# Side work of an RWKV-7 branch in fewer, larger steps: where pieces of it stand between the projection matmuls

## The chip, the cores and the metric

The kernel runs on one core of one Trainium2 chip. The metric is the device time of one execution in microseconds (us). Five engines work beside each other, each on its own queue of instructions in a fixed order: PE (TensorE, matmuls; PEld is its weight load), DVE (VectorE), ACT (ScalarE), POOL (GpSimd) and SP (SyncE, which here issues weight loads). An engine whose next instruction waits holds everything behind it.

## The reference

One decoder layer for x of 256 rows and 2048 columns, float32. A normalised x is projected once into all inputs of two branches, RWKV-7 time mixing (16 heads of 64) and block-sparse attention ("MoBA", 16 heads of 64); both are gated, projected to 2048, merged with sigmoid gates, and one output projection is added to x. The part that the change touches is the recurrence of RWKV-7. Cut to what matters:

```python
def step(state, inp):
    r_t, w_t, k_t, v_t, kk_t, b_t = inp
    sa = jnp.einsum('bhvk,bhk->bhv', state, -kk_t)
    state = (state * w_t[:, :, None, :] + sa[..., None] * b_t[:, :, None, :]
             + v_t[..., None] * k_t[:, :, None, :])
    y_t = jnp.einsum('bhvk,bhk->bhv', state, r_t)
    return state, y_t
_, y = lax.scan(step, state0, xs)
# group norm of y per head, then:
bonus = jnp.sum(rh * kh * r_k.reshape(H, N), axis=-1, keepdims=True) * vh
```

The kernel does not run 256 steps: it works in 4 chunks of 64 rows. For a chunk it needs the products of all keys with all receivers inside the chunk (key products), the inverse of a triangular matrix made of them, the values and keys transposed, and the sum over a head for the bonus (head sums).

## The kernel before

**Jobs.** The weights are float32 and each is split into a high part (`hi`) and the rest (`lo`), so that a product of precision takes three matmuls. The unit is a job: one half of a 1 MB weight load (`raw`, two buffers, one load feeds two jobs). For a job ACT makes `hi` (L216), DVE makes `lo = raw - hi` (L222), and PE runs 24 matmuls of 256 columns (L329) or 12 of 512 (L347 to L349). `hi` and `lo` have three buffers each. 258 jobs follow each other, numbered from 0: first the RWKV inputs of head group g=0 (heads 0 to 7) and attention's inputs, jobs 0 to 49; the same for g=1, jobs 50 to 97; then gates from job 98 on (98 to 129 with L329), the projections of the branches and the output projection. `run_jobs(look)` prepares job i (load, `hi`, `lo`) two jobs ahead of the one whose matmuls it issues, and after the matmuls of each job it calls `pump()`.

**Side work.** Everything else is written as Python generators in one queue, `rwkv_elem`, `rwkv_r`, `rwkv_mid`, `rwkv_v` for RWKV and `moba` for attention, per head group. `pump()` takes one step, up to the next `yield`, of the generator that stands first. So a `yield` sets how much side work is written between two jobs. A scheduler that knows dependencies and buffers then orders the instructions per engine; it can place a piece inside the matmuls of a job or some jobs away. Two steps written as one are written into one gap.

**The generators at the change.** `rwkv_r` makes the key products: for each of four feature tiles `fi` 8 matmuls into two PSUM tiles (L534; each shows as two in the trace), which DVE copies under a mask into `LL` (L538), and a `yield`. Then 16 small DMAs from ACT's queue write blocks of `LL` to DRAM (`gd`, L549), and one DMA gathers them into `sg` (L551), 64 small matrices of 32 by 32. `inverse` solves these with 31 pairs of DVE instructions on `tmp` and `kk` (L566, L569), two pairs a step; the first pair waits for `sg`. It ends with a DMA to DRAM, `td` (L573), and four that bring it back in another layout, `cs` (L578). `merge` uses `cs`: DVE transposes (L586), PE products (L595), ACT copies, PE products again. `rwkv_tr` runs in step with `inverse` (`zipped`: one step of each per gap): transposes of values on PE (L622), copied by ACT into `UV` (L628); head sums on PE (L401), multiplied with the values by DVE into `yaT` (L635, L639); transposes of keys on PE (L645), copied by ACT into `BK` (L647). It had 2 + 2 + 3 steps beside 20 of `inverse`. `rwkv_mid` is one step, then the two together, then `merge`.

**PSUM.** All small results use the pool `psd` with four buffers (tag `ps`); a fifth tile waits until the first has been read. The main matmuls have four of their own (`pm`).

Of the kernel before, what the change touches and what calls it, by code (L numbers as in the profile page):

```python
# [36 lines left out]
def tile_hybrid_block(ctx: ExitStack, tc: tile.TileContext, x, pv, wdu, wau,  # L37
# [13 lines left out]
    def nm(s):  # L51
        cnt[0] += 1
        return f"{s}_{cnt[0]}"

    def T(tag, shape, dt=F32, bufs=1):
        return sb.tile(shape, dt, tag=tag, name=nm(tag), bufs=bufs)
# [4 lines left out]
    def PSS():  # L61
        return psd.tile([P, 512], F32, tag="ps", name=nm("ps"))
# [4 lines left out]
    def f32(ap):  # L67
        return ap.bitcast(F32)
# [327 lines left out]
    def head_sums(ps, parts, half):  # L396

        for i in range(2):
            fs = slice((2 * half + i) * S, (2 * half + i + 1) * S)
            for u in range(2):  # L400
                pe.matmul(ps[:, i * S:(i + 1) * S], bones, parts[u][:, fs], start=(u == 0),  # L401
                          stop=(u == 1))
# [108 lines left out]
    def rwkv_r(g):  # L511
        r = R[g]
        rr, k, ep, ar, bk = r["r"], r["k"], r["ep"], r["ar"], r["bk"]
        dve.tensor_tensor(ar[:, :, :, 1, :], rr.rearrange("p f (c t) -> p f c t", c=4),
                          ep[:, :, :, 1:65], ALU.mult)
        yield
        for fi in range(4):
            col = 4 * g + fi
            dve.scalar_tensor_tensor(rr[:, fi, :], rr[:, fi, :], PV[:, PV_RK + col:PV_RK + col + 1],
                                     k[:, fi, :], ALU.mult, ALU.mult)  # L520
        yield
        rv = rr.rearrange("p f t -> p (f t)")
        rh, rl = T("a", [P, 1024], F32R), T("cs", [P, 1024], F32R)
        act.activation(rh, rv, AF.Copy)
        dve.tensor_tensor(rl, rv, f32(rh), ALU.subtract)
        r["rr"] = (rh, rl)
        yield
        for fi in range(4):

            pss = [PSS() for _ in range(2)]  # L530
            for c in range(4):
                for p in range(2):
                    sl = slice(64 * p, 64 * p + 64)
                    pe.matmul(pss[p][:, c * P:(c + 1) * P],  # L534
                              bk[sl, fi, c].rearrange("p a t -> p (a t)"),
                              ar[sl, fi, c].rearrange("p a t -> p (a t)"), start=True, stop=True)
            for p in range(2):
                dve.copy_predicated(  # L538
                    LL[p][:, fi].rearrange("p c a t -> p c (a t)"),
                    m2.rearrange("p a t -> p (a t)").rearrange("p (o t) -> p o t", o=1)  # L540
                    .to_broadcast([P, 4, P]),
                    pss[p].rearrange("p (c t) -> p c t", c=4))
            yield
        G = T("sg", [64, 32, 32])
        gd = dp.tile([4, 4, 4, 32, 32], F32, tag="gd", name=nm("gd"))
        for b in range(4):
            h = b % 2
            for fi in range(4):
                act.dma_start(gd[b, fi].rearrange("c s t -> s c t"),  # L549
                              LL[b // 2][32 * b:32 * b + 32, fi, :, 0, 32 * h:32 * h + 32])  # L550
        act.dma_start(G, gd.rearrange("b f c s t -> (b f c) s t"))  # L551
        Ti = T("kk", [64, 32, 32])
        pool.memset(Ti, 0.0)
        pool.memset(Ti.rearrange("p a b -> p (a b)")[:, 0:1024:33], 1.0)
        r["G"], r["Ti"] = G, Ti
# [55 lines left out]
    def rwkv_tr(g):  # L611
        r = R[g]
        v, bk, rr = r["v"], r["bk"], r["r"]
        UV = T("UV", [P, 4, 2, 4, 64])
        BK = T("BK", [P, 3, 512])
        r["UV"], r["BK"] = UV, BK
        pool.memset(UV[0:64, :, 0], 0.0)
        pool.memset(UV[64:128, :, 1], 0.0)
        for cp_ in range(2):
            ps = PSS()  # L620
            for fi in range(4):
                pe.transpose(ps[:, fi * P:(fi + 1) * P], v[:, fi, cp_ * P:(cp_ + 1) * P], ident)  # L622
            p4 = ps.rearrange("q (f p e) -> q f p e", f=4, p=2)
            for cc in range(2):
                sl = slice(64 * cc, 64 * cc + 64)
                for p in range(2):
                    so = slice(64 - 64 * p, 128 - 64 * p)
                    act.activation(UV[so, 2 * cp_ + cc, p], p4[sl, :, p, :], AF.Copy)  # L628
            yield
        for half in range(2):  # L630
            ps = PSS()
            fs = slice(2 * half, 2 * half + 2)
            head_sums(ps, r["rr"], half)
            ya = yaT[:, 4 * g + 2 * half:4 * g + 2 * half + 2, :]
            dve.tensor_tensor(ya.rearrange("p f t -> p (f t)"),  # L635
                              v[:, fs, :].rearrange("p f t -> p (f t)"), ps, ALU.mult)
            for i in range(2):
                col = 4 * g + 2 * half + i
                dve.tensor_scalar(ya[:, i, :], ya[:, i, :], PV[:, PV_GB + col:PV_GB + col + 1], None,  # L639
                                  ALU.add)  # L640
            yield
        for c in range(3):
            ps = PSS()
            for fi in range(4):
                pe.transpose(ps[:, fi * P:(fi + 1) * P],  # L645
                             bk[:, fi, c].rearrange("p a t -> p (a t)"), ident)
            act.activation(BK[:, c, :], ps, AF.Copy)  # L647
            yield

    def zipped(a, b):  # L650
        live = [a, b]
# [9 lines left out]
    def rwkv_mid(g):  # L661
        yield
        yield from zipped(inverse(g), rwkv_tr(g))
        yield from merge(g)
# [373 lines left out]
    for g in range(2):  # L1038
        c = 512 * g
        chunk(w_in, C_K + c, 512, KT, fm_x, shift_post("k", "k", g, PV_MUK, 8))  # L1040
        post = shift_post("r", "r", g, PV_MUR, 0)
        if g == 0:
            chunk(w_in, C_WD, 128, KT, fm_x, then(wa_post, (rwkv_elem(0), "e0")))
        else:
            post = then(post, (rwkv_elem(1), "e1"))
        chunk(w_in, C_R + c, 512, KT, fm_x, then(post, (rwkv_r(g), f"r{g}")))
        vp = then(shift_post("v", "v", g, PV_MUV, 16), (rwkv_mid(g), f"i{g}"), (rwkv_v(g), f"v{g}"))
        chunk(w_in, C_V + c, 512, KT, fm_x, with_need("v0", vp) if g else vp)
        qp = qk_post("q", g)
        chunk(w_in, C_Q + c, 512, KT, tm_x, with_need("m0", qp) if g else qp)  # L1050
        chunk(w_in, C_KQ + c, 512, KT, tm_x, qk_post("k", g))
        chunk(w_in, C_VQ + c, 512, KT, tm_x, then(vq_post(g), (moba(g), f"m{g}")))
# [63 lines left out]
```

## Time and profile before

| | |
|---|---|
| three runs | 831.91 us median, 829.71 to 832.96 |
| profiled execution, whole time | 834.34 us |
| its span, first to last instruction | 832.6 us |
| mean granted TensorE clock | 0.999 of full speed |
| busy PE, DVE, ACT, POOL | 819.9, 551.9, 417.8, 29.9 us |
| DMA | 145.78 MB, 175 GB/s mean |

A busy share says how much of the span an engine worked. The timeline gives each instruction with the idle time of its engine ahead of it and what ended that; a small arrow names the releaser. For an engine that is busy nearly all the time, the brackets are what is left to gain, and the room in front of other brackets is what can be lost. "ACTq" and "SPq" rows are DMAs being issued by those engines, not their transfers.

### The profile page before, as it was taken

The numbers are of one execution on the slowest core, as the hardware profiler recorded it, in microseconds if no ns is written. First come the engines' busy times: TensorE is split into PE (matmuls) and PEld (weight loads), VectorE is DVE, ScalarE is ACT, GpSimd is POOL, SyncE is SP. The second block draws the span as 40 slices with busy tenths as digits, with TensorE's granted clock in tenths as the row PEclk, the third lists the DMA queues.
The fourth block names the chain that finished last, engine by engine and source line by source line (L and its number), as shares of the span: only waits on it lengthen the run. The fifth ranks groups of instructions, "written<-read, shape, count | busy, mean of one in ns | idle before, by whom it ended". The sixth has DMA issues, their size and how long they took to land.

```text
span 832.6 us, 15909 instructions
## 1 busy us (share of the span) xinstructions
PE 819.9 (98%) x6770; PEld 764.4 (92%) x6770; DVE 551.9 (66%) x776; ACT 417.8 (50%) x565; POOL 29.9 (4%) x42
## 2 busy tenths in 40 slices
PE   8999999999999999999999999999999999999998
PEld 7999778899998888999999999999999999998887
DVE  5869958956569679649974588644445566665453
ACT  6785446444437784444444487444344444443332
POOL 5001100000000003000000000000000000000000
PEclk9999999999999999999999999999999999999999
DMA  8564554654434544655673424655555555556772
GB/s 305 181 201 152 180 166 160 202 177 153 136 119 131 174 146 137 210 140 178 203 228 106 149 66 143 224 189 172 198 194 169 195 193 166 199 182 202 248 232 97
DMA packets 83206, 145.78 MB, mean 175 GB/s; under 512 B 11568, under 2 KB 13872, under 8 KB 83136
## 3 DMA queue, kind: packets, MB, share of 16 engines
q1 hardware_dynamic: 71584, 138.55, 51.2%
q10 hardware_dynamic: 11520, 6.16, 2.8%
q8 instruction: 53, 0.87, 0.4%
q14 instruction: 17, 0.14, 0.0%
q0 software_dynamic: 32, 0.05, 0.0%
HBM read 141.61 MB, written 3.15 MB: 174 GB/s over the span
## 4 chain that ended last, share of the span: by engine, by line
PE 90%; DMA 3%; DVE 3%; ACT 2%; issue 1%; ACTq 0%; SPq 0%; DVEq 0%
PE pm L329 55%; PE pm L348 9%; PE pm L347 9%; PE pm L349 9%; PE ps L534 1%; PE ps L672 1%; PE ps L679 1%; DMA cs<-td 1%; DMA sg<-gd 1%; DVE lo L222 1%; DMA td<-kk 1%; PE ps L878 1%; DMA raw<-in_w_in_dram 1%; PE ps L696 1%; PE ps L831 1%
## 5 line engine op out<-in xcount | busy, mean ns | idle before, releaser
L222 DVE TENSOR_TENSOR lo<-raw,hi 128x1024 fp32r<-128x1024 f32 (+1 forms) x259 | 314.4, 1217 | 211.8 <-ACT hi L216 210.9
L216 ACT ACTIVATE hi<-raw 128x1024 fp32r<-128x1024 f32 (+1 forms) x259 | 272.4, 1055 | 343.9 <-PE pm L329 195.9
L329 PE MATMUL pm<-xh,hi 128*128 128x256 f32 x1168 | 329.0, 283 | 1.1 <-ACT xh L144 1.1
L329 PE MATMUL pm<-xh,lo 128*128 128x256 f32 x1168 | 325.4, 280 | 3.6 <-DVE lo L222 3.6
L329 PE MATMUL pm<-xl,hi 128*128 128x256 f32 x1168 | 326.1, 280 | 0.0
L329 PEld LDWEIGHTS pm<-xh,hi 128*128 128x128 f32 x1168 | 221.2, 190 | 4.5 <-ACT xh L144 1.5
L329 PEld LDWEIGHTS pm<-xh,lo 128*128 128x128 f32 x1168 | 219.8, 189 | 4.7 <-DVE lo L222 4.5
L329 PEld LDWEIGHTS pm<-xl,hi 128*128 128x128 f32 x1168 | 219.7, 189 | 0.5
L348 PE MATMUL pm<-lo,xh 128*128 128x512 f32 x192 | 76.5, 398 | 0.0
L349 PE MATMUL pm<-hi,xl 128*128 128x512 f32 x192 | 75.5, 393 | 0.0
L347 PE MATMUL pm<-hi,xh 128*128 128x512 f32 x192 | 72.6, 398 | 0.0
L348 PE MATMUL pm<-lo,mgh 128*128 128x512 f32 (+1 forms) x128 | 48.4, 378 | 0.0
L349 PE MATMUL pm<-hi,mgl 128*128 128x512 f32 (+1 forms) x128 | 48.1, 376 | 0.0
L347 PE MATMUL pm<-hi,mgh 128*128 128x512 f32 (+1 forms) x128 | 44.4, 378 | 0.0
L348 PEld LDWEIGHTS pm<-lo,xh 128*128 128x128 f32 x192 | 36.1, 188 | 8.0 <-DVE lo L222 0.8
L349 PEld LDWEIGHTS pm<-hi,xl 128*128 128x128 f32 x192 | 36.1, 188 | 7.3
L347 PEld LDWEIGHTS pm<-hi,xh 128*128 128x128 f32 x192 | 35.9, 188 | 7.5
L347 PEld LDWEIGHTS pm<-hi,mgh 128*128 128x128 f32 x128 | 24.1, 188 | 4.7
L349 PEld LDWEIGHTS pm<-hi,mgl 128*128 128x128 f32 x128 | 24.0, 188 | 4.7
L348 PEld LDWEIGHTS pm<-lo,mgh 128*128 128x128 f32 x128 | 24.1, 188 | 4.4
L566 DVE TENSOR_TENSOR tmp<-sg,kk 64x31 f32<-64x31 f32 (+15 forms) x62 | 20.5, 330 | 10.4 <-DMA sg<-gd 9.2
L329 PE MATMUL pm<-bk,hi 128*128 128x256 f32 x128 | 22.8, 281 | 0.0
(275 smaller groups left out, 983.5 us busy)
## 6 DMA issues: line engine op xcount, KB each, us to landing
raw<-in_w_in_dram SPq DMA_DIRECT2D x94, 1024.0 KB, 5.1
raw<-in_w_out_dram SPq DMA_DIRECT2D x16, 1024.0 KB, 5.4
raw<-in_w_proj_moba_dram SPq DMA_DIRECT2D x8, 1024.0 KB, 5.1
raw<-in_w_proj_rwkv_dram SPq DMA_DIRECT2D x8, 1024.0 KB, 5.1
raw<-in_w_in_dram SPq DMA_DIRECT2D x5, 512.0 KB, 6.1
k<-in_x_dram ACTq DMA_DIRECT2D x4, 256.0 KB, 4.0
r<-in_x_dram ACTq DMA_DIRECT2D x4, 256.0 KB, 4.2
k<-in_x_dram SPq DMA_DIRECT2D x2, 256.0 KB, 4.9
```

Of the source, the lines that this page charges most:

```text
L216: act.activation(job["hi"][:, c], job["src"][:, c], AF.Copy)
L222: dve.tensor_tensor(job["lo"][:, c], job["src"][:, c], f32(job["hi"][:, c]), ALU.subtract)
L329: pe.matmul(o, (hi, hi, lo)[ps][:, i, cs], (mh, ml, mh)[ps](k), start=(k == 0 and fi % 2 == 0 and ps == 0), stop=(k == jb["last"] and ps = ...
L347: pe.matmul(o, sh[:, k, ts], hi[:, i, cs], start=(k == 0), stop=False)
L348: pe.matmul(o, sh[:, k, ts], lo[:, i, cs], start=False, stop=False)
L349: pe.matmul(o, sl[:, k, ts], hi[:, i, cs], start=False, stop=end)
L534: pe.matmul(pss[p][:, c * P:(c + 1) * P], bk[sl, fi, c].rearrange("p a t -> p (a t)"), ar[sl, fi, c].rearrange("p a t -> p (a t)"), start= ...
L566: dve.tensor_tensor(tv, gcol.to_broadcast([64, nt, j + 1]), trow.to_broadcast([64, nt, j + 1]), ALU.mult)
L672: pe.matmul(ps[64 * p:64 * p + 64, c0 + 64 * fi:c0 + 64 * fi + 64], LL[p][:, fi, c, which, :], UV[:, c, p, fi, :], start=(fi == 0), stop=( ...
L679: pe.matmul(ps[sl, c0 + 64 * fi:c0 + 64 * fi + 64], ar[sl, fi, c, which, :], St[sl, fi, :], start=False, stop=True, skip_group_check=True)
L696: pe.matmul(ps[sl, cols], X64[sl, fi * 4 + c, :], Zs[sl, cols], start=True, stop=True)
L831: pe.matmul(pss[p][:, i * nk:(i + 1) * nk], q[rows, fi, 0:P] if u == 0 else q[rows, fi, P:S], k[rows, fi, 0:nk], start=True, stop=True)
```

## The change

Three `yield`s move. In `rwkv_r` the step ends after two feature tiles in place of one, so that four PSUM tiles of key products are written in one gap and the generator has 5 steps in place of 7. In `rwkv_tr` the two transposes of values, the two head sums and the three transposes of keys are one step each: 3 steps in place of 7. As `inverse` still has 20 steps and runs beside it, `rwkv_mid` has as many steps as before. No instruction's work is changed. Behind L543 the lines of the changed kernel are one higher (L552 there is L551 here).

```diff
@@ rwkv_r @@
                     pss[p].rearrange("p (c t) -> p c t", c=4))
-            yield
+            if fi % 2:
+                yield
         G = T("sg", [64, 32, 32])
@@ rwkv_tr @@
                     act.activation(UV[so, 2 * cp_ + cc, p], p4[sl, :, p, :], AF.Copy)
-            yield
+        yield
         for half in range(2):
...
                 dve.tensor_scalar(ya[:, i, :], ya[:, i, :], PV[:, PV_GB + col:PV_GB + col + 1], None,
                                   ALU.add)
-            yield
+        yield
         for c in range(3):
...
             act.activation(BK[:, c, :], ps, AF.Copy)
-            yield
+        yield
```

Where instructions stand now is seen in the order per engine. First ACT's queue for g=1, before, around the gather `sg` (`hi` of jobs 106, 107 and 108; the number behind a name tells buffers apart):

```order
L549 DMA gd_3889<-LL_7_120 32x4x32 x2
L549 DMA gd_3889<-LL_8_121 32x4x32 x2
L216 ACTIVATE hi_3912<-raw_3818 128x1024
L216 ACTIVATE hi_3959<-raw_3818 128x1024
L551 DMA sg_3888<-gd_3889 64x1024
L628 ACTIVATE UV_3946<-ps_3950 64x256 x4
L216 ACTIVATE hi_4013<-raw_3910 128x1024
```

The same place now; the `hi` rows are those of jobs 101, 102, 103 and 104:

```order
L216 ACTIVATE hi_3744<-raw_3623 128x1024
L550 DMA gd_3773<-LL_8_121 32x4x32
L550 DMA gd_3773<-LL_7_120 32x4x32 x2
L550 DMA gd_3773<-LL_8_121 32x4x32
L550 DMA gd_3773<-LL_7_120 32x4x32 x2
L550 DMA gd_3773<-LL_8_121 32x4x32 x3
L216 ACTIVATE hi_3796<-raw_3688 128x1024
L552 DMA sg_3772<-gd_3773 64x1024
L216 ACTIVATE hi_3852<-raw_3688 128x1024
L629 ACTIVATE UV_3830<-ps_3834 64x256 x4
L629 ACTIVATE UV_3830<-ps_3843 64x256 x4
L216 ACTIVATE hi_3904<-raw_3794 128x1024
```

The gather stands behind one `hi` where it stood behind two, and both sets of copies of values stand together behind the next.

DVE at the start of the inverse of g=1, before (`lo` of jobs 106, 107, 108; L170 and the `k` rows belong to gates):

```order
L222 TENSOR_TENSOR lo_3914<-raw_3818,hi_3912 128x1024
L222 TENSOR_TENSOR lo_3961<-raw_3818,hi_3959 128x1024
L566 TENSOR_TENSOR tmp_3940<-sg_3888,kk_3907 64x31
L170 TENSOR_TENSOR k_3987<-pm_3666,rbc 128x512
L569 TENSOR_TENSOR kk_3907<-kk_3907,tmp_3940 64x31
L170 TENSOR_TENSOR k_3987<-pm_3667,rbc 128x512
L566 TENSOR_TENSOR tmp_3943<-sg_3888,kk_3907 64x60
L569 TENSOR_TENSOR kk_3907<-kk_3907,tmp_3943 64x30x2
L222 TENSOR_TENSOR lo_4015<-raw_3910,hi_4013 128x1024
```

And now (`lo` of jobs 103 and 104 at the ends; L636 is the multiplication of the head sums):

```order
L222 TENSOR_TENSOR lo_3854<-raw_3688,hi_3852 128x1024
L567 TENSOR_TENSOR tmp_3824<-sg_3772,kk_3791 64x31
L570 TENSOR_TENSOR kk_3791<-kk_3791,tmp_3824 64x31
L567 TENSOR_TENSOR tmp_3827<-sg_3772,kk_3791 64x60
L570 TENSOR_TENSOR kk_3791<-kk_3791,tmp_3827 64x30x2
L567 TENSOR_TENSOR tmp_3880<-sg_3772,kk_3791 64x87
L570 TENSOR_TENSOR kk_3791<-kk_3791,tmp_3880 64x29x3
L567 TENSOR_TENSOR tmp_3883<-sg_3772,kk_3791 64x112
L636 TENSOR_TENSOR yaT<-v_3028,ps_3886 128x512
L570 TENSOR_TENSOR kk_3791<-kk_3791,tmp_3883 64x28x4
L636 TENSOR_TENSOR yaT<-v_3028,ps_3894 128x512
L222 TENSOR_TENSOR lo_3906<-raw_3794,hi_3904 128x1024
```

Seven small instructions of the inverse and the first multiplication now stand between the wait for `sg` and the point where the PSUM tile of the first head sums is read. On PE the key transposes of g=1 stood one set at a time, with a job's matmuls between (ahead of and behind the first of three):

```order
L329 MATMUL pm_4018<-xl,hi_4013 128x256
L329 MATMUL pm_4018<-xh,lo_4015 128x256
L645 MATMUL ps_4135<-ident,bk_3597 128x128 x4
L329 MATMUL pm_4017<-xh,hi_4057 128x256
L329 MATMUL pm_4017<-xl,hi_4057 128x256
```

Now all three stand between the matmuls of job 102 (`hi_3796`) and of job 103 (`hi_3852`):

```order
L329 MATMUL pm_3695<-xl,hi_3796 128x256
L329 MATMUL pm_3695<-xh,lo_3798 128x256
L646 MATMUL ps_3938<-ident,bk_3563 128x128 x4
L646 MATMUL ps_3944<-ident,bk_3563 128x128 x4
L646 MATMUL ps_3950<-ident,bk_3563 128x128 x4
L329 MATMUL pm_3694<-xh,hi_3852 128x256
```

The third of them takes the PSUM buffer that the first head sums had. Last, ACT at the end of the inverse of g=1, before (`hi` of jobs 126 to 129):

```order
L216 ACTIVATE hi_4681<-raw_4619 128x1024
L216 ACTIVATE hi_4713<-raw_4619 128x1024
L573 DMA td_4545<-kk_3907 64x1024
L216 ACTIVATE hi_4779<-raw_4679 128x1024
L578 DMA cs_4547<-td_4545 32x16x32 x4
L216 ACTIVATE hi_4843<-raw_4679 128x1024
```

And now (`hi` of jobs 121 to 124):

```order
L216 ACTIVATE hi_4524<-raw_4436 128x1024
L216 ACTIVATE hi_4554<-raw_4494 128x1024
L574 DMA td_4429<-kk_3791 64x1024
L216 ACTIVATE hi_4586<-raw_4494 128x1024
L579 DMA cs_4431<-td_4429 32x16x32 x4
L946 ACTIVATE qsq_4615<-qkn_4614 128x512
L216 ACTIVATE hi_4661<-raw_4552 128x1024
```

Before, `td` stood behind the second `hi` of one weight load (`raw_4619` twice); now it stands behind the first of one (`raw_4494`), and the second follows.

## Rows read from the trace of the kernel before

**Rows 1.** The profile page, busy time by engine, and granted clock in 40 slices

```profile
PE 819.9 (98%) x6770; PEld 764.4 (92%) x6770; DVE 551.9 (66%) x776; ACT 417.8 (50%) x565; POOL 29.9 (4%) x42
...
PEclk9999999999999999999999999999999999999999
```

**Rows 2.** Timeline of PE: start us, us, instruction, idle before and its releaser

```profile
374.81 0.39 PE L329 MATMUL pm<-xh,lo 128*128 128x256 f32 x1 [1.75 <-DVE lo L222]
...
382.36 0.39 PE L329 MATMUL pm<-xh,lo 128*128 128x256 f32 x1 [0.91 <-DVE lo L222]
...
186.23 1.17 PE L595 MATMUL ps<-cs,LL 32*32 32x32 f32 x32 [0.46 <-DMA cs<-td]
...
432.80 2.11 PE L595 MATMUL ps<-cs,LL 32*32 32x32 f32 x64
```

**Rows 3.** Timeline of DVE at the start of the inverse, g=1 and g=0

```profile
371.75 0.18 DVE L566 TENSOR_TENSOR tmp<-sg,kk 64x31 f32<-64x31 f32 x1 [6.22 <-DMA sg<-gd]
...
373.55 1.21 DVE L222 TENSOR_TENSOR lo<-raw,hi 128x1024 fp32r<-128x1024 f32 x1
...
127.07 0.18 DVE L566 TENSOR_TENSOR tmp<-sg,kk 64x31 f32<-64x31 f32 x1 [3.01 <-DMA sg<-gd]
```

**Rows 4.** Timeline of ACT's queue, small DMAs and the gather

```profile
360.21 1.76 ACTq L549 DMA_DIRECT2D gd<-LL  x4
...
365.56 0.47 ACTq L551 DMA_DIRECT2D sg<-gd  x1
...
123.33 0.48 ACTq L551 DMA_DIRECT2D sg<-gd  x1
```

**Rows 5.** Timeline of SP's queue, the weight loads issued near these

```profile
365.55 0.37 SPq L235 DMA_DIRECT2D raw<-in_w_in_dram  x1
...
124.09 0.37 SPq L235 DMA_DIRECT2D raw<-in_w_in_dram  x1
...
172.78 0.37 SPq L235 DMA_DIRECT2D raw<-in_w_in_dram  x1
...
420.58 11.81 SPq L235 DMA_DIRECT2D raw<-in_w_in_dram  x3
...
425.96 0.37 SPq L235 DMA_DIRECT2D raw<-in_w_in_dram  x1
```

**Rows 6.** Timeline of ACT's queue and DVE, end of the inverse, g=0 and g=1

```profile
173.65 0.48 ACTq L573 DMA_DIRECT2D td<-kk  x1
...
178.84 2.59 ACTq L578 DMA_DIRECT2D cs<-td  x4
...
184.27 0.70 DVE L586 STREAM_TRANSPOSE X<-cs 32x512 f32<-32x512 f32 x1 [5.80 <-DMA cs<-td]
...
424.52 0.47 ACTq L573 DMA_DIRECT2D td<-kk  x1
...
427.45 2.12 ACTq L578 DMA_DIRECT2D cs<-td  x4
...
431.91 1.42 DVE L586 STREAM_TRANSPOSE X<-cs 32x512 f32<-32x512 f32 x2
```

**Rows 7.** The chain that ended last: start us, us, engine, tile, line

```profile
7.79 4.68 PE pm L329 x24
12.47 0.87 PE ps L139 x8
...
19.87 2.83 PE pm L329 x24
...
114.68 1.09 PE ps L534 x16
```

**Rows 8.** Instructions by line: count, ns min/median/max, first to last start us

```profile
L538 DVE COPY_PREDICATED LL<-m,ps x16: 718/728/747, 94.7 to 360.1; 128x512 f32<-128x512 uint8 x16
...
L566 DVE TENSOR_TENSOR tmp<-sg,kk x62: 182/350/417, 127.1 to 424.0; 64x31 f32<-64x31 f32 x4, 64x60 f32<-64x60 f32 x4, 64x87 f32<-64x87 f32 x4, 64x112 f32<-64x112 f32 x4
...
L635 DVE TENSOR_TENSOR yaT<-v,ps x4: 670/672/673, 133.7 to 379.4; 128x512 f32<-128x512 f32 x4
```

## The prediction

> **What bounds the kernel now.** I read the page first, then the timeline of PE for its brackets, then DVE, ACT's queue and SP's queue around each bracket that the change can reach. On the page PE is busy 819.9 us, 98% of the span, at a granted clock in the top tenth throughout [rows 1]. The reader is to see that no amount of DVE or ACT work saved moves the end: the change alters no instruction's work, so PE's 819.9 us stay, and only PE's idle time can change. In the stretch that the change reaches it is small: 1.75 and 0.91 us at the first step of g=1's inverse, where PE waits for a `lo`, and 0.46 us in g=0's merge, where it waits for `cs` [rows 2]. Together 3.12 us. What attention waits for lies outside, and I leave it out on both sides.
>
> The cause of the first two stands on DVE: its first instruction of g=1's inverse waits 6.22 us for the gather `sg` [rows 3], and the `lo` of job 108, queued behind it, ends at 373.55 + 1.21 = 374.76, right before PE goes on at 374.81 [rows 2, 3]. So a DVE wait is free until it eats the lead that `lo` has on PE; g=0's same wait of 3.01 us left no bracket on PE [rows 3].
>
> How long a gather takes is the number that all hangs on. For g=1 it was issued at 365.56, 0.01 us behind a 1 MB weight load, and the first use came at 371.75: 6.19 us. For g=0 it was issued at 123.33, 0.76 us ahead of a load, and the use came at 127.07: 3.74 us [rows 3 to 5]. The same pair at the inverse's end: `td` issued 0.87 us behind a load (172.78) went to 178.84 before `cs` could be issued, 5.19 us, and `cs` another 5.43 to 184.27; `td` at 424.52, between loads (the row of three starts at 420.58, the next alone at 425.96), took 2.93, and `cs` at most 4.46, to 431.91 [rows 5, 6]. I call these the slow and the short price. The Trainium skill ("DMA: Bandwidth & Descriptors", section "Issuing engines are not separate DMA queues") says that transfers issued by ScalarE and SyncE end up on the same 16 engines and interleave; the trace agrees, 6.19 against 3.74.
>
> **The change part by part.** The joined steps add nothing and remove nothing; the cost of each is in what it now stands beside.
>
> *Key products.* Four PSUM tiles in one gap fill all four buffers of `psd`, so four copies of 0.73 us [rows 8] come in a row on DVE, and 16 products twice take 2 x 1.09 us on PE [rows 7]. PE itself does not wait for them. What moves is the gather. Call the start of job 98's matmuls in g=1 T0. ACT has `hi` of job 100 ready at about T0+2.1 (an estimate, good to about 1, from when the buffer of the load two ahead of it comes free), DVE its `lo` 1.2 later, two copies end at 4.75; ACT's next `hi`, of job 101, stands behind the small DMAs that need these copies and ends near 6.35; `lo` at 7.6; then the last four copies to 10.4. The last small DMAs are issued by 11.9 (four take 1.76 [rows 4]) and land 3.5 later: before, the last issue ended at 360.21 + 1.76 = 361.97 and the gather went at 365.56 [rows 4]. So `sg` is issued near T0+15.4 and lands at 19.1 by the short price, 21.6 by the slow one.
>
> *Transposes and head sums.* PE meanwhile does five jobs of 2.83, the products 2.18, value transposes 0.87 (eight, as the chain's eight [rows 7]), head sums about 0.94 (an estimate: eight matmuls and a start), and the first eight key transposes, and stands before the third set at 5 x 2.83 + 2.18 + 0.87 + 0.94 + 0.87 = T0+19.0. The third set needs the PSUM buffer of the first head sums, which DVE reads only behind the wait for `sg`, seven small instructions (0.18 to 0.42 us each [rows 8], about 1.75) and its own multiplication of 0.67 [rows 8]. So the buffer is free at 19.1 + 1.75 + 0.67 = 21.5, and PE waits about 2.4 us. This is a wait that before does not have: there each set of key transposes came a job later than the last and found its buffer read. What is queued behind the waiting transposes is job 103 and all that follows; `lo` of job 104 stands on DVE behind the second multiplication and is ready near 21.5 + 0.25 + 0.67 + 1.21 = 23.6, while job 103 ends at 21.5 + 0.3 + 2.83 = 24.6, so the second old bracket (0.91) is not paid again. Term A: 2.66 goes, 2.4 comes; bounds 0 (all covered, if the estimate of the load is 2.5 late) and 5.0 (the slow price, 2.45 more).
>
> For g=0 the first pair of tiles is copied before the rest, so the gather goes earlier against the same key transposes, and `moba` lies between. The same sum leaves 0.2 us (term B: bounds 0 and 2.4, the size of A if its margin is gone).
>
> *The merges.* As `rwkv_r` is two steps shorter, everything behind it comes two gaps earlier for g=0 and four for g=1. A weight load serves two jobs, so this turns round which inverse ends beside a load. For g=0 `td` now stands behind the second `hi` of a load, as g=1's did before, and 5.19 + 5.43 us become about 2.93 + 4.46: the 0.46 goes (term C: 0; bounds 0 and 2.6). For g=1 it stands behind the first. Before, the room from `td` to PE's product was 432.80 - 424.52 = 8.28 us, and 2.93 + 4.46 = 7.39 fitted in it [rows 2, 6]. Now the room is about the same, and 5.19 + 5.43 = 10.62 do not fit: PE waits 10.62 - 8.28 = 2.3 us (term D: bounds 0 and 2.6). The copies of values on ACT, now eight in a row where four stood, delay the next `hi`; the lead of `hi` hides that, as it hid the four, and without it the delay would fall into A's upper bound.
>
> The sum: 2.4 + 0.2 + 0 + 2.3 = 4.9 against 3.12, so +1.8. The profiled execution took 834.34 around a span of 832.6, and would take about 836.1; it stands 2.4 over the median of the runs, so I put the same +1.8 on that: 831.91 + 1.8 = 833.7.
>
> **The rivals.** (1) The waits are covered. If both gathers go at the short price and PE is a little later at its third key transposes, A, B, C and D are near 0.1 each: 0.3 in all, 3.12 - 0.3 = 2.8 saved, 829.1. For it: four gaps less between key products and merge leave more of `moba` behind as cover, and the lead on `lo` swallowed g=0's 3.01. Against it: the order puts seven inverse instructions ahead of the read that frees the buffer.
>
> (2) Slower: the gather lands late. It is the place of term A, and it decides from 7.3 us of new idle, that is from an issue beside a weight load. At the slow price A is 5.0 and the sum 7.5, 4.4 more than before: 836.3. If the slow price holds at every place, B 2.4, C 2.6 and D 2.6 make 12.6, 9.5 more: 841.4. For it: one load goes out every two jobs, 2 x 2.83 us, and two of the four places in the trace were slow. Against it: the estimate has `sg` between two loads.
>
> (3) The clock falls in a longer wait. The granted clock stays in its top tenth across the 1.75 us bracket [rows 1, 2], the 2.4 GHz level; a wait of 2.4 to 5 is not in this stretch. What a spell at the lower level would cost I bound by the kernel's first job, which comes right after PE's first idle time and took 4.68 for the 24 matmuls that later take 2.83 [rows 7], 1.85 more, though the clock row does not show a lower level there [rows 1]. One such job on top of the forecast gives 835.5; two of them with A at 5.0 give 833.7 + 2.6 + 3.7 = 840.0. The Trainium skill ("TensorE: Matmul & The Clock Gate", section "Part 1: The HAM clock gate (the "warmup" mystery)") has it that the array's clock is gated down unless there is recent work; by that rule alone a long wait is paid twice. The trace shows no fall after 1.75 us.
>
> (4) The joined steps do not stay joined, since the scheduler may spread them over the old gaps: 831.9. The order speaks against it at g=1, where three sets of key transposes stand in one gap; g=0's first pair of key products was spread.
>
> **How the numbers follow.** Forecast 0.52, covered 0.22, late gather 0.16, clock 0.06, not joined 0.04. What a measurement of this kernel can tell from no change is about 0.5%, 4.16 us: 827.75 to 836.07. Each case has about 2 us of its own on each side, as the three runs lie 829.71 to 832.96 and my estimate of T0+2.1 is good to 1. Faster by more than that is a quarter of the covered case: 0.06. Slower is a tenth of the forecast (0.05), three quarters of the late gather (0.12) and above half of the clock case (0.04): 0.21. The rest, 0.73, is within. The range goes from 828.5, leaving out a third of the covered case, to 838.0, leaving out half of the late gather and a third of the clock case, under 0.2 in all; the forecast's own range is 831.7 to 835.7.
>
> **What would show it.** After the change PE's idle before an `lo` at job 108 is gone, and a bracket of about 2.4 us stands before the third key transposes of g=1 with DVE's multiplication as its releaser (term A right); DVE's wait for `sg` in front of it is there in any case. If it reads 5, the gather was beside a load. A bracket with releaser `cs<-td` at g=1's merge of about 2.3 and none at g=0's shows C and D; `td` to `cs` near 5.2 and 2.9 us, the reverse of now, would show why. A granted clock under 1.00 behind one of the brackets would show rival 3. The prediction is wrong if PE's busy time itself changes, if brackets appear in attention or the gates that are not there now, or if the sum of the brackets named is far from 4.9.

## The result, and the profile after

The changed kernel takes 839.24 us (median of 6 runs, 836.52 to 842.54) against 831.90 of the kernel before (6 runs, 829.71 to 834.66): ratio 1.0082, 95% interval 1.0053 to 1.0112. The forecast was 833.7 and its range ended at 838.0. The profiled execution took 840.20 us around a span of 838.5. Of all runs in this document one, of e2, took 2836.97 us and is left out of its ratio.

The page after, busy time by engine and granted clock in 40 slices, beside [rows 1]:

```profile
PE 824.1 (98%) x6770; PEld 769.1 (92%) x6770; DVE 552.4 (66%) x776; ACT 416.6 (50%) x563; POOL 29.3 (3%) x42
...
PEclk9999999999999999999989999999999999999999
```

The same 6770 matmuls are busy 4.2 us longer, and one slice of the clock reads 8. So PE did not only wait, it also ran slower. This is not of the profiled execution alone: the mean granted clock is on record for every run, and lies between 0.993 and 0.996 in the six of the changed kernel, between 0.996 and 1.000 in the 67 of the kernel before that ran beside the experiments. PE's timeline after, the brackets of the stretch that the change reaches (start, us, instruction, idle before and its releaser):

```profile
124.96 0.66 PE L646 MATMUL ps<-ident,bk 128*128 128x128 f32 x4 [0.66 <-DVE yaT L636]
...
323.71 0.50 PE L348 MATMUL pm<-lo,xh 128*128 128x512 f32 x1 [0.64 <-DVE lo L222]
...
327.44 0.50 PE L348 MATMUL pm<-lo,xh 128*128 128x512 f32 x1 [0.70 <-DVE lo L222]
...
359.98 0.66 PE L646 MATMUL ps<-ident,bk 128*128 128x128 f32 x4 [0.53 <-ACT UV L629]
361.55 0.66 PE L646 MATMUL ps<-ident,bk 128*128 128x128 f32 x4 [0.91 <-ACT UV L629]
362.67 1.12 PE L646 MATMUL ps<-ident,bk 128*128 128x128 f32 x4 [0.46 <-DVE yaT L636]
...
423.87 1.90 PE L596 MATMUL ps<-cs,LL 32*32 32x32 f32 x32 [2.08 <-DMA cs<-td]
```

Together 5.98 us, where [rows 2] had 3.12. The two waits of g=1's inverse and that of g=0's merge are gone; the others are new. Windows of PE after, behind the key transposes and behind the merge (stretch: us, busy us and matmuls, granted clock, DMA share, GB/s):

```profile
360.00:364.00 4.00, 2.62 (x14) 0.81 0.79 256
364.00:368.00 4.00, 4.00 (x28) 0.76 0.02 6
368.00:372.00 4.00, 4.00 (x36) 1.00 0.79 262
...
420.00:424.00 4.00, 1.92 (x19) 0.99 1.04 299
424.00:428.00 4.00, 4.00 (x42) 0.50 0.01 1
428.00:432.00 4.00, 4.00 (x50) 0.66 0.66 193
```

At both groups of waits the clock drops to 0.50, the 1.2 GHz level, and comes back some 3.5 and 7 us later. Two rows show what that does to one matmul: its record grows from 0.28 to 0.42 us, and the next starts 0.21 behind it in place of 0.12.

```profile
364.01 0.42 PE L329 MATMUL pm<-xh,lo 128*128 128x256 f32 x1
...
366.04 0.28 PE L329 MATMUL pm<-xh,hi 128*128 128x256 f32 x1
```

ACT's queue, SP's queue and DVE after, at the end of g=1's inverse, beside [rows 5, 6]:

```profile
412.85 0.47 ACTq L574 DMA_DIRECT2D td<-kk  x1
...
418.38 2.65 ACTq L579 DMA_DIRECT2D cs<-td  x4
```

```profile
412.28 0.37 SPq L235 DMA_DIRECT2D raw<-in_w_in_dram  x1
...
418.00 0.37 SPq L235 DMA_DIRECT2D raw<-in_w_in_dram  x1
...
423.85 0.70 DVE L587 STREAM_TRANSPOSE X<-cs 32x512 f32<-32x512 f32 x1 [4.62 <-DMA cs<-td]
```

`td` is issued 0.57 behind a weight load and takes 5.53 to `cs`; `cs` goes 0.38 behind the next and takes 5.47. The forecast had put 5.19 and 5.43 there.

DVE after, in g=1's value projection of attention, where no wait was forecast:

```profile
319.36 2.03 DVE L490 TENSOR_TENSOR ar<-kk,ep 128x1024 f32<-128x1024 f32 x1
321.31 1.21 DVE L499 SCALAR_TENSOR_TENSOR a<-kk,a 128x1024 f32<-128x1024 f32 x1
322.45 1.21 DVE L222 TENSOR_TENSOR lo<-raw,hi 128x1024 fp32r<-128x1024 f32 x1
323.58 0.24 DVE L394 RECIPROCAL ssk<-ssk 128x16 f32<-128x16 f32 x1
323.75 2.39 DVE L507 TENSOR_TENSOR bk<-a,cs 64x1024 f32<-64x1024 f32 x2
326.16 1.22 DVE L222 TENSOR_TENSOR lo<-raw,hi 128x1024 fp32r<-128x1024 f32 x1
```

The `lo` of jobs 93 and 94 stand behind 3.24 and 2.63 us of `rwkv_elem` of g=1, and end at 323.66 and 327.38, right before PE goes on. That generator comes two gaps earlier too, since g=0's key products are two steps shorter.

### The profile page after: what moved, and what is told of

Same layout as the page of the kernel before. It is cut to its first block, busy times and chain, and to the rows that moved or that the text cites. A ratio compares the mean times of both kernels' runs of the same rounds, so it can differ in the third digit from the quotient of the medians.

```text
span 838.5 us, 15913 instructions
## 1 busy us (share of the span) xinstructions
PE 824.1 (98%) x6770; PEld 769.1 (92%) x6770; DVE 552.4 (66%) x776; ACT 416.6 (50%) x563; POOL 29.3 (3%) x42
## 4 chain that ended last, share of the span: by engine, by line
PE 90%; DMA 4%; DVE 3%; issue 1%; ACT 1%; ACTq 0%; SPq 0%; DVEq 0%
PE pm L329 58%; PE pm L348 8%; PE pm L349 8%; PE pm L347 8%; DMA raw<-in_w_in_dram 2%; PE ps L673 1%; DVE lo L222 1%; PE ps L680 1%; PE ps L832 1%; PE ps L879 1%; PE ps L864 1%; DMA gd<-LL 1%; DMA td<-kk 1%; DMA cs<-td 1%; PE ps L596 1%
## 5 line engine op out<-in xcount | busy, mean ns | idle before, releaser
L329 PEld LDWEIGHTS pm<-xl,hi 128*128 128x128 f32 x1168 | 223.9, 192 | 0.7 <-issue 0.2
```

Source lines behind the costliest of these rows:

```text
L329: pe.matmul(o, (hi, hi, lo)[ps][:, i, cs], (mh, ml, mh)[ps](k), start=(k == 0 and fi % 2 == 0 and ps == 0), stop=(k == jb["last"] and ps = ...
```

## The experiments

Executions of one kernel differ ahead of the change too: job 26 starts between 85.1 and 87.7 us. So beside the times I read one stage from each profiled execution, from the start of job 26's matmuls to that of job 150's; the change works inside it. Each ratio is to runs of the kernel before on the same chip: their median is 831.90 for the changed kernel, 832.37 for e1 to e4, 832.40 for e5 to e8 and 832.58 for e9.

| kernel | median, us | ratio to before, 95% | stage, us |
|---|---|---|---|
| before | 831.90 | | 438.0 |
| before, again (e12) | one run, 830.57 | | 435.1 |
| changed | 839.24 | 1.0082, 1.0053 to 1.0112 | 444.4 |
| changed, again (e8) | 836.96 | 1.0062, 1.0037 to 1.0087 | 444.1 |
| e1 products joined | 836.19 | 1.0039, 1.0022 to 1.0057 | 441.1 |
| e2 transposes joined | 837.13 | 1.0052, 1.0026 to 1.0077 | 437.4 |
| e11 the same again | one run, 837.87 | | 441.7 |
| e3 merge later | 835.51 | 1.0048, 1.0030 to 1.0066 | 437.9 |
| e10 the same again | one run, 835.83 | | 440.7 |
| e5 all joined, two steps more | 830.17 | 0.9985, 0.9969 to 1.0001 | 434.6 |
| e6 products joined, two steps more | 831.57 | 1.0000, 0.9983 to 1.0017 | 438.4 |
| e7 keys apart | 836.99 | 1.0056, 1.0034 to 1.0078 | 441.1 |
| e9 keys apart, merge later | 836.11 | 1.0040, 1.0027 to 1.0052 | 441.0 |

**e1: key products alone.**

```diff
+            if fi % 2:
+                yield
-            yield
```

> Only the key products are joined (the step ends after two feature tiles); values, head sums and key transposes stay one per step. Theory 1, the side work comes earlier: everything behind the products comes 2 and 4 gaps earlier, which brings two waits for lo in g=1's value projection of attention (0.64 + 0.70 us idle in the changed kernel) and the transfer td beside a weight load (2.08 us idle, and about 2.9 of matmuls at a granted clock of 0.5), and takes away g=1's wait at the inverse (2.66) and the 0.46 of g=0: 1.3 + 5.0 - 3.1 = about 3 us slower than before, 835. Theory 2, the joined transposes carry it all: then this kernel is at 831.9 within 1, with no clock under 1.00 between 350 and 440 us.

Measured: 3 to 4 us slower, as theory 1 has it; the waits for `lo` (0.64 and 0.70) and for `cs` are there, with the clock down behind the latter. Two more waits for a `lo` came that theory 1 did not have, 0.76 us right behind the joined products and 0.53 beside the inverse. PE's merge and the window behind it:

```profile
421.45 1.91 PE L596 MATMUL ps<-cs,LL 32*32 32x32 f32 x32 [2.25 <-DMA cs<-td]
```

```profile
422.00:426.00 4.00, 4.00 (x38) 0.50 0.00 0
```

**e2 and e11: transposes and head sums alone**, two executions profiled.

```diff
-            yield
+        yield
```

(after the values, the head sums and the keys in `rwkv_tr`)

> Only rwkv_tr is joined (values, head sums and keys one step each); the key products stay one feature tile a step, so nothing behind them comes earlier. Theory 1: no waits for lo in the value projection, no td beside a load; what is left is the wait before g=1's key transposes. They stand ahead of job 107 here and the gather behind the hi of job 107, so the wait should be longer than in the changed kernel: the gather lands near 371.7 as before, the buffer is read some 2.4 later, and PE arrives near 369: about 5 us idle and 2 to 4 of slow matmuls, less the 2.66 of before: 4 to 6 slower, 836 to 838. Theory 2 (the joined transposes carry the whole difference of the changed kernel as it is): 7.3 slower, 839.2, with a wait at both ends. If the parts simply add up, it is 839.2 less what the products alone cost, about 836.

> One more execution of the kernel with only rwkv_tr joined, whose runs stood 4.8 over before while its profiled stage (job 26 to 150) took 437.4 against 438.0. Theory 1 (its waits vary with where the weight loads fall against the gathers): another sum of waits, with the key transposes' wait above the 1.19 us of the first look. Rival: the same trace again.

Measured: 4 to 5 slower. No waits for `lo` in the value projection, but waits before the third key transposes and, which theory 1 had ruled out, before the merge: 3.35 us in e2 and 1.76 in e11. The two executions differ in the way theory 1 of e11 said: the third key transposes waited 1.03 us in e2 and 3.01 in e11. e11's queues show what goes with it: the gather went 0.06 ahead of a weight load and was used 5.77 later; in e2 it went 0.23 ahead and took 3.87.

```profile
363.57 0.48 ACTq L551 DMA_DIRECT2D sg<-gd  x1
...
363.63 0.37 SPq L235 DMA_DIRECT2D raw<-in_w_in_dram  x1
...
369.34 0.18 DVE L566 TENSOR_TENSOR tmp<-sg,kk 64x31 f32<-64x31 f32 x1 [5.73 <-DMA sg<-gd]
...
372.14 1.02 PE L645 MATMUL ps<-ident,bk 128*128 128x128 f32 x4 [3.01 <-DVE yaT L635]
```

The merge in e2:

```profile
436.50 1.37 PE L595 MATMUL ps<-cs,LL 32*32 32x32 f32 x32 [3.35 <-DMA cs<-td]
```

Each half of the change alone costs 3 to 5 us; they do not add up. That fits `td`, which both have beside a load (0.57 behind one in e1, 0.16 in e2), so that its wait is paid once; why it came there in e2, whose `rwkv_r` has its 7 steps, is not settled. The 5 us expected before the key transposes were not reached: 1.03 and 3.01.

**e3 and e10: g=1's merge two steps later**, two executions profiled.

```diff
         yield from zipped(inverse(g), rwkv_tr(g))
+        for _ in range(2 * g):
+            yield
```

> The changed kernel with two empty steps between g=1's inverse and its merge, so that PE comes to the products with cs later. Theory 1 (the wait for cs costs twice, as idle time and as slow matmuls behind it): 2.08 idle and about 2.9 of matmuls at half clock both go, 839.2 - 5.0 = 834.2, and the granted clock between 420 and 432 us is 1.00. Rival, the low clock there has another cause (what went before it, the DMA load): only the idle goes, 837.1, and the clock stays under 1.00 there.

> One more execution of the kernel with the merge two steps later. Its runs were 4.0 us over before, its profiled execution took 437.9 from job 26 to 150, as before's 438.0. Theory 1 (the wait before the key transposes is followed by half clock in some executions and not in others): the clock falls behind the key transposes this time, near 362 us, and the stage is 1.5 to 2.5 longer. Rival: the same clean trace, and the stage at 438.

Measured: in e3 the wait for `cs` is gone, and so is the low clock behind it; the stage is 6.4 shorter than the changed kernel's. In e10 the wait is back, and the low clock with it. Windows of e3 and then of e10, and e10's bracket:

```profile
420.00:424.00 4.00, 4.00 (x79) 1.00 0.28 44
424.00:428.00 4.00, 3.75 (x66) 1.00 0.39 91
```

```profile
360.00:364.00 4.00, 2.62 (x22) 1.00 0.80 262
...
424.00:428.00 4.00, 4.00 (x25) 0.57 0.17 25
```

```profile
422.04 2.11 PE L596 MATMUL ps<-cs,LL 32*32 32x32 f32 x64 [2.16 <-DMA cs<-td]
```

The edit does less than the expectation has it. In PE's order it moves the first products with `cs` by 20 of a job's 24 matmuls, 20 x 0.12 = 2.4 us, and not by two jobs; the order of ACT and DVE up to there is that of the changed kernel. `td` goes 0.37 behind a load in both, and `cs` then takes 4.70 in e3 and 6.92 in e10: 2.4 us are room enough for the one and not for the other. With `cs` nearly as late in e8 (7.16), where the products stand as in the changed kernel, PE waited 4.09 where e10 waited 2.16; about that is what the edit gives.

The expected place of the low clock in e10 (behind the key transposes) was wrong; there it stayed at 1.00, and in e3 too. Up to these transposes both kernels have the changed kernel's order, so that this part of e3's 6.4 is the scatter of executions and not the edit. The median fell by less than 5 us, and the ratio, 1.0048, is not told apart from e8's 1.0062; the mean clock of e3's 12 runs lies between 0.994 and 1.000, which fits runs of both kinds.

**e4: waits for `lo` of five sizes, in the kernel before**, in the gates, where no side work is.

```diff
+        extra = {156: 4 * [704], 164: 5 * [512], 172: 6 * [512], 180: 5 * [768], 188: 5 * [896]}
...
                 split_lo(jb)
+                for w in extra.get(i, ()):
+                    dve.tensor_tensor(jb["lo"][:, 0:w], jb["src"][:, 0:w], f32(jb["hi"][:, 0:w]),
+                                      ALU.subtract)
```

> The kernel before with some repeated DVE subtractions behind the lo of five jobs of the gates (156, 164, 172, 180, 188), where there is no side work, so that PE must wait for a lo: by rows, 4 of 0.85 us, 5 of 0.62, 6 of 0.62, 5 of 0.92, 5 of 1.07, with one or two lo of 1.21 between, less the lead of 3.49, should be idle times of about 1.1, 2.0, 2.7, 3.5 and 4.3 us. Theory 1 (an idle time of 2 us or more is followed by matmuls at half clock): behind the later four the granted clock reads 0.50 for a while, each costs some 1.5 to 3 us beyond its idle time, and the time is 832 + 13.6 + 6 to 12 = 852 to 858. Rival (the clock fell for another reason): the clock stays at 1.00 and the time is 845.5.

Measured: 849.07 (2 runs), ratio 1.0199, 1.0160 to 1.0238. PE's brackets (lines are 5 higher), and windows behind the second, third and fifth:

```profile
538.85 0.38 PE L334 MATMUL pm<-xh,lo 128*128 128x256 f32 x1 [0.88 <-DVE lo L272]
...
563.43 0.39 PE L334 MATMUL pm<-xh,lo 128*128 128x256 f32 x1 [2.53 <-DVE lo L272]
...
588.69 0.38 PE L334 MATMUL pm<-xh,lo 128*128 128x256 f32 x1 [3.22 <-DVE lo L272]
...
616.10 0.38 PE L334 MATMUL pm<-xh,lo 128*128 128x256 f32 x1 [3.75 <-DVE lo L272]
...
644.48 0.46 PE L334 MATMUL pm<-xh,lo 128*128 128x256 f32 x1 [3.99 <-DVE lo L272]
```

```profile
564.00:568.00 4.00, 4.00 (x38) 1.00 0.79 262
...
588.00:592.00 4.00, 3.31 (x21) 0.75 0.54 154
...
644.00:648.00 4.00, 3.52 (x17) 0.58 0.51 137
```

The clock fell behind 3.22, 3.75 and 3.99 us of idle time, and not behind 0.88 and 2.53. So a wait for a `lo` alone, with no small matmuls near, is enough to bring it down. But theory 1's "2 us or more" is refuted by the second: the idle time before one instruction does not tell whether the clock falls. The sum of the brackets is 14.4 us. From the start of job 150 to the last matmul PE took 321.2 us here and 303.7 in both profiled executions of the kernel before, which leaves 321.2 - 303.7 - 14.4 = 3.1 us for three falls, 1 us each and less than I had allowed.

**e5: the whole change, and two empty steps behind the key products.**

```diff
         r["G"], r["Ti"] = G, Ti
+        for _ in range(2):
+            yield
```

> The whole change, and two empty steps behind the key products of each head group, so that rwkv_r has 7 steps again: what stands behind the products comes as early as before, while the gather has two gaps more. Theory 1 (the cost is in where the pieces land, not in their being joined): no waits for lo in g=1's value projection, the gather lands well ahead of the key transposes, so that their wait is under 1 us where it was 1.9 and the 2.66 of before is gone too, and cs has about 11 us where 10.6 to 11 are needed: 832 - 2.7 + 0.5 to 1.5 = 830 to 831, granted clock 1.00 throughout. Rival (three sets of key transposes in one gap wait for PSUM buffers wherever they stand): 2 us idle and slow matmuls behind it remain, 833 to 835.

Measured: as theory 1 has it, but for two small waits. All three joined parts are in it, the order has three sets of key transposes in one gap, and the stage is 9.7 us shorter than in the changed kernel. The clock is 1.00 in every 10 us window but the last, its mean is 0.998 or more in all 12 runs, and PE has two small brackets in the stretch, right behind the joined products:

```profile
356.60 0.38 PE L329 MATMUL pm<-xh,hi 128*128 128x256 f32 x1 [0.42 <-ACT hi L216]
...
357.86 0.38 PE L329 MATMUL pm<-xh,lo 128*128 128x256 f32 x1 [0.76 <-DVE lo L222]
```

So beside these 1.2 us joining the steps costs nothing in itself here; the loss of the changed kernel is in where what follows comes to stand. At the merge it was close: `cs` was used 9.53 behind `td`, and PE came to it 9.69 behind, not 11. The kernel has the lowest ratio of all here, and is not told apart from the kernel before: the interval reaches 1.0001.

**e6: the key products joined, with the same two steps.** The diff is that of e1 and e5 together.

> Only the key products joined, with the same two empty steps. Theory 1: all stands as before but for the gather, which goes two gaps ahead of its use; the 1.75 and 0.91 us that PE waited at g=1's inverse go, nothing comes: 832.4 - 2.7 = 829.7. Rival (the wait only moves, or the merge, which comes two jobs earlier on PE here, meets cs late): 832 or above.

Measured: no gain, the rival. Theory 1's "nothing comes" failed: one wait came beside g=0's merge and two behind the joined products, 2.31 us together, and most of [rows 2]'s waits were not there to be saved (e12). In the profiled execution there is also 0.25 of waiting for `cs` and a low clock behind it, which most runs of this kernel do not show: the mean clock is 0.999 or 1.000 in 11 of 12.

```profile
178.96 0.38 PE L329 MATMUL pm<-xh,lo 128*128 128x256 f32 x1 [0.87 <-DVE lo L222]
...
358.57 0.39 PE L329 MATMUL pm<-xh,hi 128*128 128x256 f32 x1 [0.68 <-ACT hi L216]
...
359.83 0.38 PE L329 MATMUL pm<-xh,lo 128*128 128x256 f32 x1 [0.76 <-DVE lo L222]
```

```profile
423.26 2.11 PE L598 MATMUL ps<-cs,LL 32*32 32x32 f32 x64 [0.25 <-DMA cs<-td]
```

```profile
424.00:428.00 4.00, 4.00 (x60) 0.70 0.17 27
```

**e7: the change without the joined keys**, and **e9: with the merge later besides.**

```diff
             act.activation(BK[:, c, :], ps, AF.Copy)
-        yield
+            yield
```

> The whole change but for the key transposes, which are one set a step again. Theory 1 (the third set waits for the buffer of the head sums behind the gather, and the half clock follows from that wait): the 1.9 us idle before g=1's key transposes, the 0.66 before g=0's and some 1.6 of slow matmuls between 362 and 366 us go, the wait for cs and its slow matmuls stay: 839.2 - 4 = 835. Rival (the late gather is then paid at a lo some jobs later): 838 to 839, with a bracket before an lo of a job from 104 on.

> The change without the joined key transposes, and with the two empty steps ahead of g=1's merge: both stretches at half clock should be away. From the profiled executions, from job 26 to job 150: 444.2 in the changed kernel, less 6.4 (merge later) and 3.3 (keys apart) = 434.5, against 438.0 before; what is left of the change's cost is the two waits for lo in g=1's value projection (1.3). Theory 1: the stage takes 434 to 437 and the whole 830 to 833, clock 1.00 to the last stage. Rival (a cost outside what the profiled executions showed, since the merge-later kernel's runs stood 4.0 over before while its profiled stage equalled before's): 835 or above with a clean trace.

> The changed kernel once more, on the same chip and beside the same runs of before as the three others: both theories expect 1.005 to 1.011 times before, about 839, and the same two stretches at half clock behind the key transposes and behind the merge's first products.

Measured: e8 is as expected, with both stretches at half clock again (0.76 from 362 to 366 us, 0.50 from 424 to 428). Against it (836.96, same chip and runs of before) e7's median is no better, 836.99, yet its stage is 3.0 shorter, near the expected 4. 1.0 of that is a shorter wait for `cs` (3.12 against 4.09), which is not the edit's. For the rest PE waits 0.47 us before the transposes and 0.57 before a `lo` soon behind (the rival's bracket, in small), where e8 has 0.38, 0.91 and 0.53, and the clock stays at 1.00; but so it did in e3 and e10 with the keys joined. So e7 shows that the wait for the buffer of the head sums goes with the joined keys, and settles neither the clock nor the price. e9 did not reach the expected 830 to 833: its stage was 441.0, because `cs` took 6.34 after a `td` 0.37 behind a load, and PE waited 1.91 with the clock at 0.50 behind it. It had the same 2.4 us of room as e3. Its rival asked for a clean trace, and this one was not clean.

**e12: the kernel before, once more.**

> One more execution of the kernel before, for the scatter of a single profiled execution: the same waits (1.75, 0.91, 0.46) in all of them, the granted clock at 1.00, the stage from job 26 to 150 at 438 within 1, and any difference of the whole ahead of job 26, where the change doesn't reach.

Measured: not the same waits: the 1.75 and the 0.46 are gone, 0.24 is left of the 0.91, and the stage is 435.1 where 438 within 1 was expected. The clock is 1.00 as expected. ACT's gather, SP's load and DVE's wait for g=1, then PE's bracket:

```profile
364.36 0.52 ACTq L551 DMA_DIRECT2D sg<-gd  x1
...
364.56 0.37 SPq L235 DMA_DIRECT2D raw<-in_w_in_dram  x1
...
367.96 0.18 DVE L566 TENSOR_TENSOR tmp<-sg,kk 64x31 f32<-64x31 f32 x1 [3.43 <-DMA sg<-gd]
...
378.58 0.38 PE L329 MATMUL pm<-xh,lo 128*128 128x256 f32 x1 [0.24 <-DVE lo L222]
```

Here the gather went 0.20 ahead of the load and took 3.60; in [rows 3 to 5] it went 0.01 behind it and took 6.19. In e4, whose order is that of before up to the gates, it went 0.22 ahead and took 3.77, with 0.20 us of waiting on PE. Of three executions of that order, one paid the 2.66 us.

## Why the prediction was wrong, point by point

**The bound, the step that failed.** "PE's 819.9 us stay, and only PE's idle time can change" was wrong. Trace against trace the stage grew by 6.3 us (438.04 to 444.35) where the forecast had +1.8. Longer waits are 2.3 of it, near the forecast; the other 4.0 are the same matmuls running slower at a granted clock of 0.50, which the sum put at nothing. (In e8, of 6.0 us, longer waits are 4.0 and slower matmuls 2.0.) The prediction named a change of PE's busy time as what would show it wrong. What was right is that idle time of PE is paid in the end.

**The credit of 2.66 us in term A, the second step that failed.** The 1.75 and 0.91 were those of one execution, whose gather went 0.01 behind a load; in e12 and e4, with the gather 0.20 and 0.22 ahead of it, 0.24 and 0.20 are paid. The execution was 2.4 over the median of the runs, and I noted that without asking what made it so. With e12 as the base, the stage of the changed kernel is 444.4 - 435.1 = 9.3 longer: waits of 5.98 against 0.24 there and 0.57 in attention that is not paid now, so 5.2, and 4.2 of slower matmuls, sum 9.4.

**Term A, what comes.** The size holds: 1.90 us of idle time where 2.4 were put (21.5 - 19.0 is 2.5). The mechanism is right for the third set of transposes (the buffer of the head sums, read behind the gather, releaser `yaT`), but the first two sets waited for ACT's copies of values (0.53 and 0.91), which stand behind the gather's issue and one more `hi`; I had said the lead of `hi` hides them. As the third set's release ends all three, the sum of 1.90 is that of the path I had followed, though only 0.46 was paid with its releaser. The gather itself took the short price in both executions of the changed kernel (3.52 and 3.59), 2.92 ahead of a load, so rival 2's condition was not met.

**Term B.** 0.66 where 0.2 was put, in its bounds, releaser as in term A.

**Terms C and D.** Right in both places: C's wait is gone with `td` to `cs` at 2.92, D's is 2.08 where 2.3 was put, with `td` beside a load as worked out. e8 shows 4.09 in the same place, since `cs` took 7.16 there: the bound of 2.6 was too narrow.

**The part that was missing.** The shift by two steps was followed for the merges and not for `rwkv_elem` of g=1, which stands behind g=0's key products in the same queue: 1.34 us of waits for `lo`. They are in every profiled kernel whose `rwkv_r` has 5 steps, and in none of e2, e5, e6, e11 and e12, where it has 7.

**Rival 3, given 0.06, is what happened**, on top of the forecast and twice. The forecast had the waits in its sum, at 2.3 and 2.4; waits longer than any of the trace should have carried a good chance of the low clock, and 1.85 for each of two makes 837.4. At the merge it came each time: in eight executions PE waited 1.76 to 4.09 us there, and the clock fell behind all eight. At the key transposes no single wait was over 0.91, so there the condition of rival 3 was not met as it was stated. The Trainium skill ("TensorE: Matmul & The Clock Gate", section "Part 1: The HAM clock gate (the "warmup" mystery)") says that the throttled state is the default and activity releases it; the windows above agree in the two levels, 1.00 and 0.50, and in the fall behind waits, while no run here shows which is the default. I had cited the rule and let the absence of a fall after 1.75 us in one trace outweigh it.

**Not settled:** why the clock fell at 0.53, 0.91 and 0.46 us of waits in the changed kernel and at 0.38, 0.91 and 0.53 in e8, and not at 0.40, 0.91 and 0.54 in e3 or 0.59, 0.92 and 0.46 in e10, where the order is the same; and why the two sets of runs of the changed kernel differ (1.0082 and 1.0062, intervals that overlap). The price of each part in the median is known to 2 us at best.

## What to carry to other kernels

In an in-order queue of side work, the length of one generator is the start time of all that follow: after changing a number of steps, follow every later piece to what it will stand beside, above all DMAs that come beside periodic loads. Take a wait as a saving only when more than one execution shows it; where two queues issue within some tenths of a microsecond of each other, price both outcomes. Where PE is the bound, price each new wait at its idle time and at the slower matmuls that can follow, and where a change shortens side work, try it with the old length kept by empty steps, which here took back all of the loss (0.9985, 0.9969 to 1.0001).

## What the runs showed of the hardware

The small transfers to and from DRAM have two prices. In 14 profiled executions `td` took 5.1 to 6.0 us to its use when it went 0.15 to 0.9 behind a 1 MB load, and 2.9 when it went 3.5 to 4.0 behind one; between, at 1.6 to 1.7, it took from 3.9 to 6.7. The gather took 3.3 to 3.9, but for the two that went within 0.06 of a load, 5.77 and 6.19. No run moved a load on purpose, so that the traces show the two going together and no more. The Trainium skill ("DMA: Bandwidth & Descriptors", section "Latency and other measured facts") has the access to HBM slower under load, 0.2 us on average and 2 us at high load; the traces agree in sign, with about 2.5 us between the two prices of a transfer, and do not show where in the transfer it goes.

A low clock also came behind 64 products of 32 by 32 with only 0.25 us of idle time before them (e6), and did not behind 2.53 us (e4), nor behind such products with no idle time before them (the kernel before, e3 and e5).
